# Silu in one activation, a third seven-product pair in every other feed-forward job, and the sums of down on VectorE

## The chip, the cores and the metric

The kernel runs on one core of one Trainium2 chip. A core has five engines with queues of their own: TensorE (PE in the rows; PEld are its weight loads), VectorE (DVE), ScalarE (ACT), GpSimd (POOL) and SyncE (SP, which here issues the loads of weights). Each takes its instructions in order. The metric is the device time of one execution, in microseconds; the time of before is the median of 3 runs.

## The reference

One decoder layer for 256 tokens of width 2048 in float32. Two mixers (a gated delta rule and a block attention) are merged by gates and projected; then comes a dense SwiGLU feed-forward, the part that the change touches:

```python
u = _rmsnorm(h, norm_ffn_w[l])
hid = jax.nn.silu(jnp.einsum('btd,df->btf', u, w_ffn_gate[l])) * jnp.einsum('btd,df->btf', u, w_ffn_up[l])
h = h + jnp.einsum('btf,fd->btd', hid, w_ffn_down[l])
```

with `D_FF` = 5632, so gate and up are 2048x5632 each and down is 5632x2048.

## The kernel before

**Float32 from three products.** TensorE multiplies operands of a shorter type (float32r). Each float32 tile is therefore held as two parts, hi (the tile cast to that type) and lo (what the cast left out). A product is three matmuls into the same bank: activation hi by weight hi (line 283), hi by lo (284), lo by hi (285). Weights come from HBM as units of 128x1024 (`wraw`). For each unit ScalarE casts `whi` (line 87) and VectorE subtracts `wlo` (line 88). Both have four buffers, and `get` asks for the parts three units ahead (`SPLIT_AHEAD`).

**Super jobs.** The feed-forward is 13 jobs: 11 for gate and up (512 columns of each side by side, `c` = 0 to 10) and 2 for down (1024 columns each). A job goes through its contraction in pairs of 128-row blocks: 8 pairs for gate and up, 22 for down. A pair is a 2x2 by 2x2 block product (two blocks of rows, two halves of the tokens, two blocks of columns). An ordinary pair needs 2 units of weights and 8 products (24 matmuls). A pair of *seven products* uses Winograd's form of Strassen's scheme: 21 matmuls on 4 units, of which two are built by VectorE from the loaded ones (lines 96, 97, 99 and 100, in place on `wraw`), one of 512 columns and three of 1024. It also needs sums of the activations: `make_sums` forms a sum of hi and lo (line 967) and four sums of quarters (970 to 973) on GpSimd, then ScalarE casts (975) and VectorE subtracts (976) the two parts. These sums are `usum` for gate and up, made once, and `dsum` for down, eight pairs. The products that seven-product pairs collect in four more banks (`pw`) are folded by `after` (lines 996 to 1000) on ScalarE and GpSimd behind the last such pair of a job.

Which pairs are of seven products, and in which order a job takes its pairs, stands in a table at the head of the program:

```python
FFN_PAIRS = (3, 5)
FFN_ORDER = [[0, 1, 2, 4, 6, 3, 5, 7]] + [list(range(KM // 2))] * (DFF // 512 - 1)
DOWN_PAIRS = (4, 8, 12, 15, 18, 2, 6, 10)
DOWN_USED = [(4, 8, 12, 15, 18), DOWN_PAIRS]
```

Job 0 thus has its two such pairs next to each other; in the other gate and up jobs pair 4 lies between 3 and 5.

**Side work.** While TensorE multiplies, short chains of other work are woven in, one step per `tick`, one or two ticks per pair's unit: `swiglu` of the job before (adds of the folded products, the activation, the products with up, 8 transposes, the split of `hid`), the sums of down, the output. The scheduler of the language then settles the order in which each engine gets its instructions; the order is fixed when the program is built. The second down job takes its last four units together (`last`).

Of the kernel before, what the change touches and what calls it, by code (L numbers as in the profile page):

```python
# [24 lines left out]
DFF = 5632  # L25
# [11 lines left out]

FFN_PAIRS = (3, 5)  # L40
FFN_ORDER = [[0, 1, 2, 4, 6, 3, 5, 7]] + [list(range(KM // 2))] * (DFF // 512 - 1)
DOWN_PAIRS = (4, 8, 12, 15, 18, 2, 6, 10)
DOWN_USED = [(4, 8, 12, 15, 18), DOWN_PAIRS]


def _super_jobs():

    jobs = [[(p, p in FFN_PAIRS) for p in order] for order in FFN_ORDER]
    return jobs + [[(p, p in used) for p in range(KF // 2)] for used in DOWN_USED]


# [61 lines left out]
def layer(ctx: ExitStack, tc: tile.TileContext, xT, xtok, params, consts, relt, w_bd, w, out):  # L113
    nc = tc.nc
# [25 lines left out]
    def small(name, shape, dtype=F32):  # L140
        return pools[-1].tile([P] + list(shape), dtype, name=name)
# [166 lines left out]
    with tc.tile_pool(name="xin", bufs=4) as xin:  # L308
# [597 lines left out]
    uT = acts.tile([P, KM, 512], F32R, name="uT", tag="actA")  # L906
# [23 lines left out]
        turn([h[:, n, fs] for n in range(NT)], weighted(j))  # L930
    low_stage.close()
    mid.close()
    r2h, r2q = small("r2h", [NT]), small("r2q", [NT])

    def h_scale():
        ss = small("hs", [NT])
        nc.vector.tensor_reduce(ss, hss, axis=AX.X, op=ALU.add)
        r2 = rsqrt("r2", ss, 1.0 / DM)
        nc.vector.tensor_scalar(r2h, r2, 0.5, None, op0=ALU.mult)
        nc.vector.tensor_mul(r2q, r2h, r2)  # L940
        yield

    chains.append(h_scale())


    low = acts.tile([P, H, 512], F32R, name="low", tag="actC")
    later = {}

    def hid(kc, n=1):
        t, k = (low, kc) if kc < H else (later["high"], kc - H)  # L950
        return t[:, k] if n == 1 else t[:, k:k + n]

    def fft(name, bufs):
        return later["ff"].tile([P, 512], F32, name=name, tag=name, bufs=bufs)
# [5 lines left out]
            nc.vector.tensor_sub(hid(4 * c, 4)[:, :, T + n * P:T + (n + 1) * P], p, hi.bitcast(F32))  # L960
        return evict

    def make_sums(g, c):

        c = c.bitcast(F32)
        f = fft("fsum", 2).rearrange("p (k t) -> p k t", k=2)
        nc.gpsimd.tensor_add(f, c[:, :, :T], c[:, :, T:])
        a11, a21, a12, a22 = f[:, 0, :P], f[:, 0, P:], f[:, 1, :P], f[:, 1, P:]
        t = fft("fsum", 2).rearrange("p (k t) -> p k t", k=4)
        nc.gpsimd.tensor_add(t[:, 0], a21, a22)  # L970
        nc.gpsimd.tensor_sub(t[:, 1], t[:, 0], a11)
        nc.gpsimd.tensor_sub(t[:, 2], a11, a21)
        nc.gpsimd.tensor_sub(t[:, 3], a12, t[:, 1])
        yield
        nc.scalar.copy(g[:, 0], t)
        nc.vector.tensor_sub(g[:, 1], t, g[:, 0].bitcast(F32))  # L976
        yield

    usums = {}

    def ffn_setup():
        by_stage.close()
        later["ff"] = ff = ctx.enter_context(tc.tile_pool(name="ff", bufs=1))
        later["high"] = ff.tile([P, KF - H, 512], F32R, name="high")
        yield
        for p in FFN_PAIRS:
            usums[p] = ff.tile([P, 2, 4, P], F32R, name="usum", tag="sum", bufs=2)
            yield from make_sums(usums[p], uT[:, 2 * p:2 * p + 2])

    parts = []  # L990

# [179 lines left out]
```

## Time and profile before

| | |
|---|---|
| median of 3 runs | 1475.7 us (1475.5 to 1476.75) |
| the profiled execution | 1475.54 us, of it 1473.8 us span of the profile |
| mean granted TensorE clock | 0.997 of full speed |
| TensorE busy | 1458.2 us, 99% of the span |
| VectorE, ScalarE, GpSimd busy | 73%, 52%, 14% |
| gate and up, then down | from about 763 us, from about 1230 us |

Durations of matmuls overlap, since they are pipelined, so their sum is no measure of how fast TensorE goes; distances between starts are.

### The profile page before, as it was taken

The numbers are of one execution on the slowest core, as the hardware profiler recorded it, in microseconds if no ns is written. First come the engines' busy times: TensorE is split into PE (matmuls) and PEld (weight loads), VectorE is DVE, ScalarE is ACT, GpSimd is POOL, SyncE is SP. The second block draws the span as 40 slices with busy tenths as digits, with TensorE's granted clock in tenths as the row PEclk, the third lists the DMA queues.
The fourth block names the chain that finished last, engine by engine and source line by source line (L and its number), as shares of the span: only waits on it lengthen the run. The fifth ranks groups of instructions, "written<-read, shape, count | busy, mean of one in ns | idle before, by whom it ended". The sixth has DMA issues, their size and how long they took to land.

```text
span 1473.8 us, 19231 instructions
## 1 busy us (share of the span) xinstructions
PE 1458.2 (99%) x7077; PEld 1213.5 (82%) x7077; DVE 1078.7 (73%) x1452; ACT 759.9 (52%) x1100; POOL 200.9 (14%) x148
## 2 busy tenths in 40 slices
PE   9999999999999999999999999999999999899998
PEld 8888788888888888888888888888888887688887
DVE  6887679777664455555569888888888887777885
ACT  6664446635454444444545555555555554444553
POOL 0011000020000000000021223022222116405003
PEclk9999999999999999999999999999999999899999
DMA  9457545575456666668756666565665556557763
GB/s 375 147 197 183 162 136 176 163 170 186 143 159 180 195 195 186 189 191 258 217 173 200 214 191 193 170 203 187 214 207 192 190 184 198 163 197 224 231 204 109
DMA packets 78735, 282.05 MB, mean 191 GB/s; under 512 B 8880, under 2 KB 9520, under 8 KB 78256
## 3 DMA queue, kind: packets, MB, share of 16 engines
q1 hardware_dynamic: 76032, 272.30, 59.3%
q0 software_dynamic: 1472, 5.24, 1.1%
q10 hardware_dynamic: 1136, 3.28, 1.0%
q8 instruction: 55, 0.90, 0.2%
q14 instruction: 40, 0.33, 0.1%
HBM read 276.46 MB, written 4.33 MB: 191 GB/s over the span
## 4 chain that ended last, share of the span: by engine, by line
PE 93%; DVE 3%; ACT 1%; issue 1%; POOL 1%; DMA 0%; SPq 0%; DVEq 0%; POOLq 0%; ACTq 0%
PE ps L283 13%; PE ps L284 13%; PE ps L285 13%; PE ps L218 11%; PE ps L219 11%; PE ps L220 11%; PE ps L199 6%; PE ps L200 3%; PE pw L284 2%; PE pw L285 2%; PE pw L283 2%; PE pT L299 1%; DVE wlo L88 1%; ACT whi L87 1%; DVE dsum L976 0%
## 5 line engine op out<-in xcount | busy, mean ns | idle before, releaser
L88 DVE TENSOR_TENSOR wlo<-wraw,whi 128x1024 fp32r<-128x1024 f32 (+1 forms) x575 | 702.8, 1236 | 282.1 <-ACT whi L87 277.0
L87 ACT CAST whi<-wraw 128x1024 fp32r<-128x1024 f32 (+1 forms) x575 | 585.3, 1025 | 604.2 <-PE ps L285 233.6
L283 PE MATMUL ps<-whi,uT 128*128 128x512 f32 x572 | 223.8, 391 | 0.7 <-ACT whi L87 0.7
L285 PE MATMUL ps<-whi,uT 128*128 128x512 f32 x572 | 222.8, 390 | 0.0
L284 PE MATMUL ps<-wlo,uT 128*128 128x512 f32 x572 | 222.8, 389 | 0.0
L218 PE MATMUL ps<-whi,aT 128*128 128x512 f32 x512 | 204.5, 400 | 0.0
L219 PE MATMUL ps<-wlo,aT 128*128 128x512 f32 x512 | 200.1, 391 | 0.1
L220 PE MATMUL ps<-whi,aT 128*128 128x512 f32 x512 | 199.8, 390 | 0.0
L199 PE MATMUL ps<-aT,whi 128*128 128x512 f32 x384 | 139.0, 405 | 1.7 <-DVE aT L333 1.7
L283 PEld LDWEIGHTS ps<-whi,uT 128*128 128x128 f32 x572 | 107.4, 188 | 23.0 <-ACT whi L87 1.1
L285 PEld LDWEIGHTS ps<-whi,uT 128*128 128x128 f32 x572 | 107.4, 188 | 22.6
L284 PEld LDWEIGHTS ps<-wlo,uT 128*128 128x128 f32 x572 | 107.4, 188 | 21.9
L220 PEld LDWEIGHTS ps<-whi,aT 128*128 128x128 f32 x512 | 96.1, 188 | 20.3
L218 PEld LDWEIGHTS ps<-whi,aT 128*128 128x128 f32 x512 | 96.3, 188 | 18.8
L219 PEld LDWEIGHTS ps<-wlo,aT 128*128 128x128 f32 x512 | 96.3, 188 | 18.5 <-DVE wlo L88 0.4
L200 PE MATMUL ps<-aT,wlo 128*128 128x256 f32 x384 | 108.4, 282 | 0.9 <-DVE wlo L88 0.9
L199 PEld LDWEIGHTS ps<-aT,whi 128*128 128x128 f32 x384 | 73.5, 192 | 18.5 <-DVE aT L333 2.0
L284 PE MATMUL ps<-wlo,high 128*128 128x512 f32 x216 | 84.7, 392 | 0.4 <-DVE wlo L88 0.4
L283 PE MATMUL ps<-whi,high 128*128 128x512 f32 x216 | 84.6, 392 | 0.0
L285 PE MATMUL ps<-whi,high 128*128 128x512 f32 x216 | 84.6, 392 | 0.0
L997 POOL TENSOR_TENSOR ft<-ft 128x512 f32<-128x512 f32 x13 | 23.5, 1805 | 446.7 <-ACT ft L996 446.7
L200 PEld LDWEIGHTS ps<-aT,wlo 128*128 128x128 f32 x384 | 73.8, 192 | 1.3 <-DVE wlo L88 1.2
(395 smaller groups left out, 2004.3 us busy)
## 6 DMA issues: line engine op xcount, KB each, us to landing
wraw<-in_w SPq DMA_DIRECT2D x503, 512.0 KB, 4.2
xrow<-in_xtok SPq DMA_DIRECT2D x1, 2048.0 KB, 13.7
lb<-dm ACTq DMA_DIRECT2D x2, 1024.0 KB
xr<-in_xtok SPq DMA_DIRECT2D x8, 256.0 KB, 6.9
hsave<-h POOLq DMA_DIRECT2D x4, 512.0 KB, 5.5
hx<-hsave POOLq DMA_DIRECT2D x4, 512.0 KB, 7.8
xc<-in_xT SPq DMA_DIRECT2D x3, 512.0 KB, 7.5
bias<-in_relt SPq DMA_DIRECT2D x4, 256.0 KB, 4.0
```

The source lines that it names most:

```text
L87: self.last_hi = self.nc.scalar.copy(hi[:, f], raw[:, f])
L88: self.last_lo = self.nc.vector.tensor_sub(lo[:, f], raw[:, f], hi[:, f].bitcast(F32))
L199: nc.tensor.matmul(ps[:, j], hi[:, sl], act[:, kc], start=kc == 0, stop=False)
L200: nc.tensor.matmul(ps[:, j, :T], lo[:, sl], act[:, kc, :T], start=False, stop=kc == nk - 1)
L218: nc.tensor.matmul(ps[n], ah, hi[:, sl], start=kc == 0, stop=False)
L219: nc.tensor.matmul(ps[n], ah, lo[:, sl], start=False, stop=False)
L220: nc.tensor.matmul(ps[n], al, hi[:, sl], start=False, stop=kc == nk - 1)
L283: nc.tensor.matmul(ps, ah, hi[:, sl], start=i == use[0], stop=False)
L284: nc.tensor.matmul(ps, ah, lo[:, sl], start=False, stop=False)
L285: nc.tensor.matmul(ps, al, hi[:, sl], start=False, stop=i == use[-1])
L299: nc.tensor.transpose(p[n][:, i], srcs[n][:, i * P:(i + 1) * P], ident)
L997: nc.gpsimd.tensor_add(t[2], t[0], t[2])
```

## The change

Three things. The gate's activation is `Silu` in one ScalarE instruction in place of `Tanh` and a VectorE instruction that made Silu of it; `r2h` and `r2q` become one `r2`. Gate and up jobs of odd number have three seven-product pairs (2, 4 and 5) in their natural order, those of even number two (2 and 5), with pair 3 taken before 2; down has six (7, 9, 11, 13, 15, 17) in its first job and these and 2 and 5 in its second. And the five operations of `make_sums` run on VectorE, in `ft` tiles for gate and up and in a tile `room2` for down, with a third buffer of the tag `sum`; the order within `make_sums` puts the cast ahead of the `yield`.

```diff
-FFN_PAIRS = (3, 5)
-FFN_ORDER = [[0, 1, 2, 4, 6, 3, 5, 7]] + [list(range(KM // 2))] * (DFF // 512 - 1)
-DOWN_PAIRS = (4, 8, 12, 15, 18, 2, 6, 10)
-DOWN_USED = [(4, 8, 12, 15, 18), DOWN_PAIRS]
+FFN_PAIRS = (2, 4, 5)
+FFN_USED = [(2, 5), (2, 4, 5)]
+FFN_ORDER = [[0, 1, 3, 4, 6, 2, 5, 7]] + [[0, 1, 2, 3, 4, 5, 6, 7], [0, 1, 3, 2, 4, 5, 6, 7]] * (DFF // 1024)
+DOWN_PAIRS = (7, 9, 11, 13, 15, 17, 2, 5)
+DOWN_USED = [DOWN_PAIRS[:6], DOWN_PAIRS]
...
-    jobs = [[(p, p in FFN_PAIRS) for p in order] for order in FFN_ORDER]
+    jobs = [[(p, p in FFN_USED[c % 2]) for p in order] for c, order in enumerate(FFN_ORDER)]
...
-        f = fft("fsum", 2).rearrange("p (k t) -> p k t", k=2)
-        nc.gpsimd.tensor_add(f, c[:, :, :T], c[:, :, T:])
+        f = f.rearrange("p (k t) -> p k t", k=2)
+        nc.vector.tensor_add(f, c[:, :, :T], c[:, :, T:])
         a11, a21, a12, a22 = f[:, 0, :P], f[:, 0, P:], f[:, 1, :P], f[:, 1, P:]
-        t = fft("fsum", 2).rearrange("p (k t) -> p k t", k=4)
-        nc.gpsimd.tensor_add(t[:, 0], a21, a22)
-        nc.gpsimd.tensor_sub(t[:, 1], t[:, 0], a11)
-        nc.gpsimd.tensor_sub(t[:, 2], a11, a21)
-        nc.gpsimd.tensor_sub(t[:, 3], a12, t[:, 1])
-        yield
+        t = t.rearrange("p (k t) -> p k t", k=4)
+        nc.vector.tensor_add(t[:, 0], a21, a22)
+        nc.vector.tensor_sub(t[:, 1], t[:, 0], a11)
+        nc.vector.tensor_sub(t[:, 2], a11, a21)
+        nc.vector.tensor_sub(t[:, 3], a12, t[:, 1])
         nc.scalar.copy(g[:, 0], t)
+        yield
         nc.vector.tensor_sub(g[:, 1], t, g[:, 0].bitcast(F32))
...
-            nc.scalar.activation(gs[n], t[2 * n], AF.Tanh, scale=r2h[:, n:n + 1])
+            nc.scalar.activation(gs[n], t[2 * n], AF.Silu, scale=r2[:, n:n + 1])
...
-            nc.vector.scalar_tensor_tensor(gs[n], gs[n], 1.0, t[2 * n], op0=ALU.add, op1=ALU.mult)
-        yield
-        for n in range(NT):
-            nc.vector.scalar_tensor_tensor(gs[n], t[2 * n + 1], r2q[:, n:n + 1], gs[n], op0=ALU.mult, op1=ALU.mult)
+            nc.vector.scalar_tensor_tensor(gs[n], t[2 * n + 1], r2[:, n:n + 1], gs[n], op0=ALU.mult, op1=ALU.mult)
...
+        room = later["ff"].tile([P, 2, 512], F32, name="room2", tag="sum", bufs=3)
         for i, p in enumerate(DOWN_PAIRS):
-            yield from make_sums(dsum[:, i], hid(2 * p, 2))
+            yield from make_sums(dsum[:, i], hid(2 * p, 2), room[:, 0], room[:, 1])
```

The line numbers of the changed program are one higher than before up to the sums, and differ by one to three behind them (88 is now 89 for `wlo`, 976 is 975, 960 is 959).

How the orders move, at three places. First, VectorE in gate and up job 1, from the split of `hid` of job 0 (`low`) on. Before, an ordinary pair's rows stand between the first seven-product pair and the second, and behind the second only ordinary weights follow:

```order
L960 TENSOR_TENSOR low<-pT,low 128x4x128 x2
L88 TENSOR_TENSOR wlo<-wraw,whi 128x1024 x3
L88 TENSOR_TENSOR wlo<-wraw,whi 128x512
L96 TENSOR_TENSOR wraw<-wraw 128x512
L88 TENSOR_TENSOR wlo<-wraw,whi 128x1024
L97 TENSOR_TENSOR wraw<-wraw 128x512
L99 TENSOR_TENSOR wraw<-wraw 128x512
L100 TENSOR_TENSOR wraw<-wraw 128x512
L88 TENSOR_TENSOR wlo<-wraw,whi 128x1024 x9
```

In the changed program, at the same place:

```order
L959 TENSOR_TENSOR low<-pT,low 128x4x128 x2
L89 TENSOR_TENSOR wlo<-wraw,whi 128x1024 x2
L89 TENSOR_TENSOR wlo<-wraw,whi 128x512
L97 TENSOR_TENSOR wraw<-wraw 128x512
L89 TENSOR_TENSOR wlo<-wraw,whi 128x1024
L98 TENSOR_TENSOR wraw<-wraw 128x512
L100 TENSOR_TENSOR wraw<-wraw 128x512
L101 TENSOR_TENSOR wraw<-wraw 128x512
L89 TENSOR_TENSOR wlo<-wraw,whi 128x1024 x2
L89 TENSOR_TENSOR wlo<-wraw,whi 128x512
L97 TENSOR_TENSOR wraw<-wraw 128x512
L89 TENSOR_TENSOR wlo<-wraw,whi 128x1024
```

The rows of pair 5 (the second group from `wlo` 128x512 on) now follow those of pair 4 directly.

Second, VectorE at the start of the first down job, from the end of `swiglu` of job 10 on. Before, it has one instruction per sum (`dsum`), and the first seven-product pair's weights (128x512, 96, 97) begin behind the third sum:

```order
L1016 SCALAR_TENSOR_TENSOR fg<-ft,r2q,fg 128x512 x2
L88 TENSOR_TENSOR wlo<-wraw,whi 128x1024
L976 TENSOR_TENSOR dsum<-fsum,dsum 128x512
L88 TENSOR_TENSOR wlo<-wraw,whi 128x1024
L976 TENSOR_TENSOR dsum<-fsum,dsum 128x512
L88 TENSOR_TENSOR wlo<-wraw,whi 128x1024
L976 TENSOR_TENSOR dsum<-fsum,dsum 128x512
L88 TENSOR_TENSOR wlo<-wraw,whi 128x512
L960 TENSOR_TENSOR high<-pT,high 128x4x128 x2
L96 TENSOR_TENSOR wraw<-wraw 128x512
L976 TENSOR_TENSOR dsum<-fsum,dsum 128x512
L97 TENSOR_TENSOR wraw<-wraw 128x512
```

In the changed program, from the same point on (`room` is the tile of the sums):

```order
L1012 SCALAR_TENSOR_TENSOR fg<-ft,r2s,fg 128x512 x2
L89 TENSOR_TENSOR wlo<-wraw,whi 128x1024
L975 TENSOR_TENSOR dsum<-room_10594,dsum 128x512
L969 TENSOR_TENSOR room_10594<-room_10594 128x128
L971 TENSOR_TENSOR room_10594<-room_10594 128x128
L970 TENSOR_TENSOR room_10594<-room_10594 128x128
L89 TENSOR_TENSOR wlo<-wraw,whi 128x1024
L972 TENSOR_TENSOR room_10594<-room_10594 128x128
L966 TENSOR_TENSOR room_10594<-high 128x512
L975 TENSOR_TENSOR dsum<-room_10594,dsum 128x512
L969 TENSOR_TENSOR room_10594<-room_10594 128x128
L971 TENSOR_TENSOR room_10594<-room_10594 128x128
```

Each sum's six VectorE instructions lie between the subtractions of ordinary weights, all eight sums ahead of the third unit of the first seven-product pair.

Third, ScalarE at the end of job 0, in the changed program:

```order
L995 COPY ft<-pw 128x512 x4
L88 CAST whi<-wraw 128x1024 x4
L1006 ACT_TABLE_LOAD
L1006 ACTIVATE fg<-ft,r2s 128x512 x2
L88 CAST whi<-wraw 128x512
```

Before, there is no table load at this place, only one at the start of the program; now there are these two in all.

## Rows read from the trace of the kernel before

**Rows 1.** Head of the profile: busy time, share of the span, instructions of TensorE.
```profile
PE 1458.2 (99%) x7077; PEld 1213.5 (82%) x7077; DVE 1078.7 (73%) x1452; ACT 759.9 (52%) x1100; POOL 200.9 (14%) x148
```

**Rows 2.** Timeline of TensorE in down: start, duration, line, operation.
```profile
1249.76 0.39 PE L283 MATMUL pw<-whi,high 128*128 128x512 f32 x1
...
1281.41 0.39 PE L283 MATMUL pw<-whi,high 128*128 128x512 f32 x1
...
1302.49 0.39 PE L283 MATMUL pw<-whi,high 128*128 128x512 f32 x1
...
1448.01 0.39 PE L283 MATMUL pw<-whi,high 128*128 128x512 f32 x1
...
1469.62 0.39 PE L285 MATMUL ps<-whi,high 128*128 128x512 f32 x1
```

**Rows 3.** Windows: stretch, length, busy us of each engine, PEclk, DMA share, GB/s.
```profile
1250.00:1266.00 16.00, 10.05 (x26) 6.40 (x25) 10.54 (x10) 5.48 (x7) 13.93 (x15) 0.68 0.27 79
1266.00:1291.00 25.00, 25.00 (x112) 20.67 (x111) 19.57 (x20) 13.45 (x15) 3.59 (x4) 1.00 0.69 210
```

**Rows 4.** All waits of TensorE after 800 us: total us, times, longest.
```profile
PE pw L284 <- DVE wlo L88: 3.3, 2, 2.6
PE ps L284 <- DVE wlo L88: 1.6, 2, 1.2
PE pw L283 <- ACT whi L87: 1.4, 1, 1.4
```

**Rows 5.** Timeline, first sums of down; in brackets idle time, releaser.
```profile
1252.05 0.50 PE L284 MATMUL ps<-wlo,dsum 128*128 128x512 f32 x1 [1.21 <-DVE wlo L88]
...
1253.29 0.62 ACT L975 CAST dsum<-fsum 128x512 fp32r<-128x512 f32 x1 [3.62 <-POOL fsum L973]
...
1253.94 1.21 DVE L976 TENSOR_TENSOR dsum<-fsum,dsum 128x512 fp32r<-128x512 f32 x1 [1.95 <-ACT dsum L975]
...
1259.54 1.23 DVE L976 TENSOR_TENSOR dsum<-fsum,dsum 128x512 fp32r<-128x512 f32 x1 [1.53 <-ACT dsum L975]
```

**Rows 6.** Groups by line and shape, VectorE: busy us, mean ns, idle before.
```profile
L88 DVE TENSOR_TENSOR wlo<-wraw,whi 128x1024 fp32r<-128x1024 f32 x538 | 678.6, 1273 | 264.1 <-ACT whi L87 259.0 <-DMA wraw<-in_w 1.5 <-PE pPT L829 0.6
...
L1013 DVE SCALAR_TENSOR_TENSOR fg<-fg,ft 128x512 f32<-128x512 f32 x22 | 14.5, 683 | 0.0
...
L606 DVE TENSOR_TENSOR prod<-lb,X 128x128 f32<-128x128 f32 x2 | 0.8, 394 | 0.1
...
L568 DVE TENSOR_TENSOR mc<-mc,cst 128x128 f32<-128x128 f32 x2 | 0.6, 280 | 0.0
```

**Rows 7.** Timelines of TensorE and VectorE in job 0, two neighbouring seven-product pairs.
```profile
779.34 0.39 PE L283 MATMUL pw<-whi,uT 128*128 128x512 f32 x1
...
787.62 0.50 PE L283 MATMUL ps<-whi,uT 128*128 128x512 f32 x1 [0.71 <-ACT whi L87]
...
809.06 1.04 PE L299 MATMUL pT<-ident,fg 128*128 128x128 f32 x8
...
780.67 1.83 DVE L88 TENSOR_TENSOR wlo<-wraw,whi 128x1024 fp32r<-128x1024 f32 x2 [0.26 <-ACT whi L87]
...
784.27 0.69 DVE L97 TENSOR_TENSOR wraw<-wraw 128x512 f32<-128x512 f32 x1
784.99 0.69 DVE L99 TENSOR_TENSOR wraw<-wraw 128x512 f32<-128x512 f32 x1
...
786.33 4.76 DVE L88 TENSOR_TENSOR wlo<-wraw,whi 128x1024 fp32r<-128x1024 f32 x4
```

**Rows 8.** The same in job 1, second seven-product pair.
```profile
822.90 0.39 PE L283 MATMUL pw<-whi,uT 128*128 128x512 f32 x1
...
824.23 3.61 DVE L88 TENSOR_TENSOR wlo<-wraw,whi 128x1024 fp32r<-128x1024 f32 x3 [0.66 <-ACT whi L87]
```

**Rows 9.** Groups by line and shape, ScalarE: busy us, mean ns, idle before.
```profile
L1007 ACT ACTIVATE fg<-ft,r2h 128x512 f32<-128x512 f32 x22 | 14.7, 715 | 3.1 <-DVE ft L1006 3.1
...
L321 ACT ACT_TABLE_LOAD x1 | 1.3, 1283 | 1.7 <-PEq L1162 1.7
```

More of the change, by code (lines that the diff above doesn't have):

```diff
@@ L932, in layer @@
     mid.close()
-    r2h, r2q = small("r2h", [NT]), small("r2q", [NT])
+    r2 = small("r2s", [NT])
     def h_scale():
@@ L937, in h_scale @@
         nc.vector.tensor_reduce(ss, hss, axis=AX.X, op=ALU.add)
-        r2 = rsqrt("r2", ss, 1.0 / DM)
-        nc.vector.tensor_scalar(r2h, r2, 0.5, None, op0=ALU.mult)
-        nc.vector.tensor_mul(r2q, r2h, r2)
+        nc.vector.tensor_copy(r2, rsqrt("r2", ss, 1.0 / DM))
         yield
@@ L961, in parted, with make_sums @@
         return evict
-    def make_sums(g, c):
+    def make_sums(g, c, f, t):
         c = c.bitcast(F32)
-        f = fft("fsum", 2).rearrange("p (k t) -> p k t", k=2)
-        nc.gpsimd.tensor_add(f, c[:, :, :T], c[:, :, T:])
+        f = f.rearrange("p (k t) -> p k t", k=2)
+        nc.vector.tensor_add(f, c[:, :, :T], c[:, :, T:])
         a11, a21, a12, a22 = f[:, 0, :P], f[:, 0, P:], f[:, 1, :P], f[:, 1, P:]
-        t = fft("fsum", 2).rearrange("p (k t) -> p k t", k=4)
-        nc.gpsimd.tensor_add(t[:, 0], a21, a22)
-        nc.gpsimd.tensor_sub(t[:, 1], t[:, 0], a11)
-        nc.gpsimd.tensor_sub(t[:, 2], a11, a21)
-        nc.gpsimd.tensor_sub(t[:, 3], a12, t[:, 1])
+        t = t.rearrange("p (k t) -> p k t", k=4)
[3 more added lines that the diff above has]
+        nc.vector.tensor_sub(t[:, 3], a12, t[:, 1])
+        nc.scalar.copy(g[:, 0], t)
         yield
-        nc.scalar.copy(g[:, 0], t)
         nc.vector.tensor_sub(g[:, 1], t, g[:, 0].bitcast(F32))
@@ L986, in ffn_setup @@
         for p in FFN_PAIRS:
-            usums[p] = ff.tile([P, 2, 4, P], F32R, name="usum", tag="sum", bufs=2)
-            yield from make_sums(usums[p], uT[:, 2 * p:2 * p + 2])
+            usums[p] = ff.tile([P, 2, 4, P], F32R, name="usum", tag="sum", bufs=3)
+            yield from make_sums(usums[p], uT[:, 2 * p:2 * p + 2], fft("ft", 4), fft("ft", 4))
     parts = []
@@ L1048, in layer @@
     for j in range(2):
-        hx = [later["ff"].tile([P, NT, 512], F32, name="hx", tag="sum", bufs=2) for _ in range(2)]
+        hx = [later["ff"].tile([P, NT, 512], F32, name="hx", tag="sum", bufs=3) for _ in range(2)]
         for f in range(2):
```

## The prediction

> **What bounds the kernel now.** I read the head of the profile first: TensorE is busy for 99% of the span [rows 1], so time can only come from fewer matmuls or from stretches in which matmuls run late. The busy figure cannot show lateness, since durations of pipelined matmuls overlap. The timeline can: count the matmuls between two points, and multiply by the undisturbed pitch. In the first down job the seven-product pairs 8 and 12 begin at 1281.41 and 1302.49 us [rows 2]; between them lie one pair of seven products (21 matmuls) and three ordinary pairs (24 each), 93 matmuls in 21.08 us, or 0.2267 us each. That is the price of a matmul here, not the 0.39 us that a row shows.
>
> The same ruler finds the late places. Pair 4 begins at 1249.76 us; from there to pair 8 there are again 93 matmuls, but they take 31.65 us [rows 2]: **10.57 us are lost at the first sums of down.** The windows agree: TensorE is busy 10.05 of 16 us there, and the mean granted clock falls to 0.68, so part of the stretch ran at the lower of its two levels, 1.2 GHz [rows 3]. Last, the list of TensorE's waits has only five after 800 us, all on weight halves (`whi`, `wlo`) [rows 4]; the first is at 1252.05 us. The timeline there says why: ScalarE's next instruction is a cast of a sum (`dsum`, L975) that waits 3.62 us for GpSimd, and VectorE's for the same sum waits 1.95 us for ScalarE [rows 5]; the weight casts (L87) and subtractions (L88) that TensorE needs are queued behind these two. One lap of this chain takes 5.6 us (1253.94 to 1259.54), too long for two laps in a seven-product pair.
>
> **The products.** An ordinary pair is 8 products of 3 matmuls, a seven-product pair 7. Now there are 11×2 + 5 + 8 = 35 such pairs; then 6×2 + 5×3 + 6 + 8 = 41. Six pairs more remove 18 matmuls: 18 × 0.2267 = **−4.08 us**.
>
> **The sums of down.** GpSimd's five operations per sum become VectorE's: one of 128x512 at 0.69 us (as L97) [rows 7] and four of 128x128. Rows of that size lie at 0.280 (L568) and 0.394 us (L606) [rows 6]; I take 0.33, the middle. A sum thus adds 2.0 us to VectorE, and the cast no longer waits for another engine's queue. The first such pair is now pair 7, not 4, so eight sums have 14 ordinary units of weights (two per pair, 12 × 0.2267 = 2.72 us each) in which to be made. Is VectorE fast enough? From the start of the job to the third unit of that pair, TensorE needs 14 × 12 + 9 = 177 matmuls, 40.1 us, and 0.9 us of transposes: 41.0 us. The order of rows gives VectorE in that stretch, at 1.18 us from start to start for a weight subtraction (four run in 4.76 us) [rows 7]: 12 of units 2 to 13 (14.2), the old job's rest (8 of 512, 5.5), eight `dsum` (5.5), six sums of 512 (4.1), 28 small ones (9.2), and the pair's own work to its third unit (5.9): 44.4 us. It starts with the first finished bank of the job before, about 1.9 us (8 matmuls) early, so it is ready at 42.5: 1.5 us late, or 0.1 if the small ones take 0.28, or 3.3 at 0.394. I take **0.7 us** of remaining wait, about halfway between the first two. So −10.57 + 0.7 = **−9.9 us**. If the sums held the queues as long as now, the gain would be 0.
>
> **The third pair in every other feed-forward job.** Jobs 1, 3, 5, 7 and 9 have pairs 2, 4 and 5, and 4 and 5 are neighbours. A seven-product pair gives TensorE 21 × 0.2267 = 4.76 us, but costs VectorE about 0.69 + 3 × 1.18 + 4 × 0.72 = 7.1 us [rows 7]. A single one is absorbed: after 800 us no job's pair made TensorE wait, as they stand one ordinary pair apart. But job 0 already has two neighbours, and there the trace shows the price. The first begins at 779.34 and the next transposes at 809.06, with 126 matmuls (42 + 24 + 60) between: 29.72 − 28.56 = **1.16 us late**, with a visible wait on `whi` at 787.62 [rows 7]. The mechanism is a chain from the four buffers of `whi`: the first pair's fourth unit cannot be cast before TensorE leaves the last ordinary unit. VectorE starts its subtraction at 780.67, 1.33 us after the pair's start, and from there works through the second pair's changes of weights to 786.33, where the third unit's subtraction starts. That is ready at 787.5, while TensorE would want it after 21 + 9 matmuls, at 786.14.
>
> Would jobs 1 to 9 be any better? In job 1 of before, the second pair's fourth unit starts on VectorE 1.33 us after that pair's start too (822.90, 824.23), with VectorE idle 0.66 us ahead of it [rows 8], after one ordinary pair, as in the change. So the chain begins at the same point with no debt, and runs the same operations in the same order. I take 1.16 us five times: **+5.8 us**. The bounds are 0, if TensorE's reordering hides it, and 2.8 us each, if VectorE's debt from the earlier pair (7.1 − 4.76 = 2.3 us) is not worked off. The third pair is therefore a bad bargain: 3.4 us of products (15 matmuls) for 5.8 us of waits. Job 0 keeps its neighbours (2 and 5 now), and its own sums, three on VectorE, fill gaps there: 0, with up to 1 us more.
>
> **Silu.** Two VectorE operations per job vanish (22 × 0.683 = 15 us of VectorE's time) [rows 6], at the start of a job, where nothing waits for VectorE now: 0 on the path. No row shows Silu; the nearest is Tanh at 0.715 us for the same shape and the same pointer scale [rows 9], and plain casts are 0.6. Even 1 us more would only shorten a margin. In ScalarE's order one table load appears, ahead of the first Silu in job 1, and none after. A load took 1.283 us at the start [rows 9]; in job 1 VectorE's second subtraction has a us of slack behind it: 0, bounded by 1.3. The Trainium skill, "ScalarE: Activation LUTs", section "What ACT_TABLE_LOAD costs", adds a drain of about 1.38 us, 2.66 us for a switch; no run here shows that drain, and by that price the same bound would be 2.7 us, once.
>
> **Nothing for the rest.** The 93 matmuls from pair 18's start (1448.01) on end at about 1469.85, one pitch after the last start, 0.76 us late [rows 2]. The change ends GpSimd's additions a pair earlier there, but the last four units are still fetched together: 0, at best −0.76. The third `sum` buffer and the earlier load of `hx` lie on GpSimd's queue, which waits for ScalarE anyway.
>
> **Sum.** −4.08 − 9.9 + 5.8 = −8.2 us. The profiled execution took 1475.54 us (span 1473.8), 0.2 below the median of the runs shown: 1475.54 − 8.2 = **1467.3 us**.
>
> **Rivals.**
> 1. *The neighbours cost nothing* (TensorE finds other matmuls, or the shorter VectorE list in these jobs helps): −4.08 − 9.9 = −14.0, so **1461.6**. Against it: job 0 has the same chain. Chance 0.14.
> 2. *VectorE is late with more than this*: with 3.3 us at the sums and 2 us for each of the five, −14.65 + 3.3 + 10 = −1.4, **1474**; milder mixes give 1470 and up. For it: 44.4 us of work in 41. Chance 0.17.
> 3. *VectorE pays for emptying its pipe behind every operation.* The timeline speaks against it: dependent operations of 0.69 us start 0.72 us apart (784.27 and 784.99 us) [rows 7]. Were each of the eight sums 1.2 us longer, 9.6 us of the gain would be lost, and the time **1476.9**. Chance 0.03. The Trainium skill, "VectorE: DVE Perf Modes", section "The DRAIN you can't avoid", states such a flush of about the operation's time less 266 ns; these rows show none between starts.
> 4. *Slower*: the waits at the neighbours let the granted clock fall, as in the first down job. It decides from (14.65 − 0.7) / 5 = 2.8 us per job. If each wait of 1.16 us also brought 16 matmuls at half the clock (16 × 0.2267 = 3.6 us more), it would be 4.8 us a job: −14.0 + 24 = +10, **1485**. Against it: job 0's 1.16 us is measured 20 us behind its wait and holds whatever the clock did; the low clock stands where four waits come together [rows 3, 4]. Chance 0.07.
>
> **Chances.** My forecast (1464.5 to 1470) has 0.55, and 0.04 lies between the cases. About 0.2%, 3 us, is what a measurement of this kernel can tell from no change. Faster takes the forecast, rival 1, the better part of rival 2 (0.1) and the rest: 0.83; same, the other part of rival 2 and most of rival 3: 0.09; slower: 0.08. The range reaches down over rival 1 and up to rival 2's worst: 1461 to 1473.
>
> **What the new profile would show.** Right: no TensorE wait between the start of down and its end but for one under 1 us at pair 7; no clock below 1.00 there; in jobs 1, 3, 5, 7, 9 one wait each on `whi` or `wlo` in pair 5, and distances that are about 1.2 us over the count; 18 matmuls fewer. Wrong: odd jobs that keep to the count; waits on `dsum` or the weight halves in the first down job; several table loads; half clock after pair 5.

## The result and the profile after

The changed kernel takes **1467.68 us** (median of 4 runs, 1467.31 to 1470.37) against 1476.14 us before (4 runs, 1475.5 to 1476.75): a ratio of 0.9947, 95% interval 0.9929 to 0.9964. The forecast was 1467.3 us. The profiled execution of the changed kernel is its longest, 1470.37 us with a span of 1468.6 us. It lost time ahead of the change: a group of four transposes of `h`, which stands 12 matmuls into gate and up job 0, starts 2.86 us later than in the profile of before, although TensorE's 3930 matmuls and transposes ahead of it are the same in both programs.

These transposes in TensorE's timeline of before:

```profile
753.80 0.60 PE L299 MATMUL pT<-ident,h 128*128 128x128 f32 x4
```

And TensorE's timeline after, from the same transposes to the last matmul, with jobs 0 and 1 and the first seven-product pair of down between, which answers to [rows 2, 7, 8]:

```profile
756.66 0.60 PE L300 MATMUL pT<-ident,h 128*128 128x128 f32 x4
...
782.18 0.39 PE L284 MATMUL pw<-whi,uT 128*128 128x512 f32 x1
...
809.19 1.03 PE L300 MATMUL pT<-ident,fg 128*128 128x128 f32 x8
...
813.95 0.50 PE L284 MATMUL pw<-whi,usum 128*128 128x512 f32 x1 [0.99 <-DVE low L959]
...
821.57 0.39 PE L284 MATMUL pw<-whi,uT 128*128 128x512 f32 x1
...
826.33 0.39 PE L284 MATMUL pw<-whi,uT 128*128 128x512 f32 x1
...
829.84 0.50 PE L284 MATMUL pw<-whi,usum 128*128 128x512 f32 x1 [0.69 <-ACT whi L88]
...
854.02 0.60 PE L300 MATMUL pT<-ident,fg 128*128 128x128 f32 x4
...
1217.30 0.39 PE L284 MATMUL pw<-whi,uT 128*128 128x512 f32 x1
...
1271.92 0.39 PE L284 MATMUL pw<-whi,high 128*128 128x512 f32 x1
...
1464.44 0.39 PE L286 MATMUL ps<-whi,high 128*128 128x512 f32 x1
```

From the first of these rows to the start of the last matmul, before takes 1469.62 [rows 2] - 753.80 = 715.82 us, after 1464.44 - 756.66 = 707.78 us: **8.04 us less, where the prediction's sum says 8.2**. I compare this stretch from here on, since it leaves out a part that the change doesn't touch and that differs between executions (what is known of it stands at the end of the account of the prediction).

With the prediction's ruler of 0.2267 us per matmul: job 0 has 114 matmuls from 782.18 to the transposes, 25.84 us, and takes 27.01, so 1.17 us are lost at its neighbours, as before. In job 1, 117 matmuls from pair 5 (826.33) on are 26.52 us and take 27.69: 1.17 lost. Job 3's (913.01 to 940.68) lose 1.15. From 1217.30 up to the first seven-product pair of down at 1271.92 there are 237 matmuls and 8 transposes, 53.73 and some 0.87 us, in 54.62: nothing is lost. The surprise is in job 1 ahead of the neighbours. The row of 813.95 lies in its first seven-product pair, which begins behind the transposes at 809.98. From there 45 matmuls, 10.20 us, take until 821.57: **1.39 us lost, once**.

The head of the profile after, which answers to [rows 1], has 18 matmuls less, 69 more instructions on VectorE and 50 fewer on GpSimd:

```profile
PE 1452.2 (99%) x7059; PEld 1207.2 (82%) x7059; DVE 1109.0 (76%) x1521; ACT 772.3 (53%) x1114; POOL 157.4 (11%) x98
```

All waits of TensorE after 780 us (total us, times, longest), which answer to [rows 4]:

```profile
PE pw L284 <- ACT whi L88: 3.5, 5, 0.7
PE pw L284 <- DVE low L959: 1.0, 1, 1.0
PE ps L284 <- ACT whi L88: 0.7, 1, 0.7
PE ps L285 <- DVE wlo L89: 0.7, 1, 0.7
```

The first row is the five odd jobs, one wait each. The third is job 0, the fourth the last units of the program; at both places before had one too. The second, on the split of `hid` (`low`), was not foreseen: those matmuls write a bank that still holds the transposes until VectorE has split them. Nothing is left in the first down job, where the windows (stretch, length, busy us of each engine, granted clock, DMA share, GB/s), which answer to [rows 3], now show a full TensorE at full clock and a VectorE with hardly a gap:

```profile
1254.00:1272.00 18.00, 18.00 (x81) 14.91 (x80) 17.72 (x36) 8.26 (x11) 0.72 (x1) 1.00 0.54 163
1272.00:1291.00 19.00, 19.00 (x86) 15.73 (x85) 17.59 (x20) 11.44 (x12) 0.00 (x0) 1.00 0.75 249
```

### The profile page after: what moved, and what is told of

Same layout as the page of the kernel before. It is cut to its first block, busy times and chain, and to the rows that moved or that the text cites. A ratio compares the mean times of both kernels' runs of the same rounds, so it can differ in the third digit from the quotient of the medians.

```text
span 1468.6 us, 19242 instructions
## 1 busy us (share of the span) xinstructions
PE 1452.2 (99%) x7059; PEld 1207.2 (82%) x7059; DVE 1109.0 (76%) x1521; ACT 772.3 (53%) x1114; POOL 157.4 (11%) x98
## 4 chain that ended last, share of the span: by engine, by line
PE 85%; DVE 6%; DMA 3%; ACT 2%; issue 2%; POOL 0%; ACTq 0%; SPq 0%; DVEq 0%; POOLq 0%
PE ps L285 13%; PE ps L286 13%; PE ps L284 13%; PE ps L219 9%; PE ps L220 9%; PE ps L221 9%; PE ps L200 5%; DMA lb<-dm 3%; PE ps L201 3%; DVE wlo L89 2%; PE pw L285 2%; PE pw L286 2%; PE pw L284 2%; ACT whi L88 2%; PE pT L300 1%
## 5 line engine op out<-in xcount | busy, mean ns | idle before, releaser
L89 DVE TENSOR_TENSOR wlo<-wraw,whi 128x1024 fp32r<-128x1024 f32 (+1 forms) x587 | 717.5, 1240 | 261.3 <-ACT whi L88 259.0
L88 ACT CAST whi<-wraw 128x1024 fp32r<-128x1024 f32 (+1 forms) x587 | 594.2, 1023 | 596.6 <-PE ps L221 228.1
L284 PE MATMUL ps<-whi,uT 128*128 128x512 f32 x542 | 212.0, 391 | 0.7 <-ACT whi L88 0.7
L286 PE MATMUL ps<-whi,uT 128*128 128x512 f32 x542 | 211.0, 389 | 0.0
L285 PE MATMUL ps<-wlo,uT 128*128 128x512 f32 x542 | 211.0, 389 | 0.0
L284 PEld LDWEIGHTS ps<-whi,uT 128*128 128x128 f32 x542 | 101.8, 188 | 21.9 <-ACT whi L88 1.1
L286 PEld LDWEIGHTS ps<-whi,uT 128*128 128x128 f32 x542 | 101.7, 188 | 21.3
L285 PEld LDWEIGHTS ps<-wlo,uT 128*128 128x128 f32 x542 | 101.8, 188 | 20.8
L286 PE MATMUL ps<-whi,high 128*128 128x512 f32 x210 | 81.7, 389 | 0.0
L284 PE MATMUL ps<-whi,high 128*128 128x512 f32 x210 | 81.5, 389 | 0.0
```

The source lines that it names most:

```text
L88: self.last_hi = self.nc.scalar.copy(hi[:, f], raw[:, f])
L89: self.last_lo = self.nc.vector.tensor_sub(lo[:, f], raw[:, f], hi[:, f].bitcast(F32))
L284: nc.tensor.matmul(ps, ah, hi[:, sl], start=i == use[0], stop=False)
L285: nc.tensor.matmul(ps, ah, lo[:, sl], start=False, stop=False)
L286: nc.tensor.matmul(ps, al, hi[:, sl], start=False, stop=i == use[-1])
```

## The experiments

All are compared over the same stretch, so that each number has a trace behind it, and by their medians. "Less" and "more" below are differences of the stretch. The kernel before ran on the same chip as each of them: 1474.01 us (9 runs) beside the first four, 1474.73 (9) beside the next four, 1474.56 (16) beside the last two.

| kernel | median us (runs) | ratio to before, 95% interval | stretch, us | against before |
|---|---|---|---|---|
| before | 1476.14 (4) | | 715.82 | |
| after | 1467.68 (4) | 0.9947, 0.9929 to 0.9964 | 707.78 | -8.04 |
| e1_two_pairs | 1462.16 (4) | 0.9918, 0.9904 to 0.9931 | 704.14 | -11.68 |
| e2_apart | 1460.37 (4) | 0.9910, 0.9895 to 0.9925 | 702.02 | -13.80 |
| e3_table_early | 1468.37 (5) | 0.9961, 0.9949 to 0.9974 | 708.83 | -6.99 |
| e4_gpsimd_sums | 1480.28 (5) | 1.0040, 1.0027 to 1.0052 | 720.96 | +5.14 |
| e5_vector_sums | 1463.80 (4) | 0.9922, 0.9907 to 0.9937 | 705.28 | -10.54 |
| e6_five_whi | 1468.05 (6) | 0.9951, 0.9936 to 0.9966 | 705.62 | -10.20 |
| e7_job0 | 1466.18 (4) | 0.9942, 0.9927 to 0.9956 | 706.88 | -8.94 |
| e8_apart_job0 | 1460.05 (4) | 0.9900, 0.9885 to 0.9914 | 701.15 | -14.67 |
| e9_silu_only | 1476.72 (11) | 1.0010, 1.0001 to 1.0019 | 717.54 | +1.72 |
| e10_three_apart | 1469.55 (6) | 0.9970, 0.9958 to 0.9981 | 710.27 | -5.55 |

**The third pair, taken away (e1).** My theory: the third pair costs more than its products give. The rival: what is lost in odd jobs is lost at the products, not at the neighbours.

```diff
-FFN_USED = [(2, 5), (2, 4, 5)]
+FFN_USED = [(2, 5), (2, 5)]
-FFN_ORDER = ... [[0, 1, 2, 3, 4, 5, 6, 7], [0, 1, 3, 2, 4, 5, 6, 7]] ...
+FFN_ORDER = ... [[0, 1, 3, 2, 4, 5, 6, 7], [0, 1, 3, 2, 4, 5, 6, 7]] ...
```

> Every gate and up job takes two seven-product pairs, 2 and 5, with one ordinary pair between them (job 0 keeps its neighbours). My theory: each of the five odd jobs loses a wait of 1.16 us and gets 3 matmuls back (0.68 us), so 5 x (1.16 - 0.68) = 2.4 us faster than the changed kernel, about 1465.2 us, and no wait on whi inside jobs 1 to 10. Rival: the wait comes with any job's seven-product pairs and not with neighbours; then the 15 matmuls come on top, 3.4 us slower, about 1471.

Measured: 3.64 us less than after. The neighbours' five waits are gone (two of 0.7 us are left, in job 0 and at the end), and job 1's wait on `low` with them, since its first seven-product pair now comes one pair later. That second effect is the excess over the forecast: five times 1.16 less 15 x 0.2267 = 3.40 gives 2.4, and job 1's 1.39 makes it 3.8, where 3.64 was measured.

**The third pair, kept but apart (e2).** The order alone decides, if neighbours are the cause:

```diff
-[0, 1, 2, 3, 4, 5, 6, 7]
+[0, 1, 2, 3, 4, 6, 5, 7]
```

> The odd jobs keep three seven-product pairs, but take pair 6 between 4 and 5 (positions 2, 4 and 6 of 8). My theory: no neighbours, no waits, so 5 x 1.16 = 5.8 us faster than the changed kernel, about 1461.9. Rival: the folded products' four additions on GpSimd (some 8.4 us behind four copies) now have only one ordinary pair, 5.4 us, until the job ends; VectorE's first add of the next job waits up to 5 us for them, and the weight subtractions queued behind it make TensorE wait: no gain, or up to 5 us a job slower (1468 to 1490).

Measured: 5.76 us less than after. The five waits are gone, job 1's is not:

```profile
PE pw L284 <- DVE low L959: 1.0, 1, 1.0
PE ps L284 <- ACT whi L88: 0.7, 1, 0.7
PE ps L285 <- DVE wlo L89: 0.7, 1, 0.7
```

So the third pair is not bad by itself. Here one ordinary pair between two seven-product pairs pays for both, as the prediction read from before; the place made it a loss.

**A fifth buffer of `whi` (e6).** The mechanism that the prediction gave for the neighbours is a chain from the four buffers of `whi`. The fifth buffer took the room of one buffer of `wraw`.

```diff
-RAW = 7
+RAW = 6
-        hi = self.pool.tile([P, 1024], F32R, name="whi", tag="whi", bufs=4)
+        hi = self.pool.tile([P, 1024], F32R, name="whi", tag="whi", bufs=5)
```

> The changed kernel with five buffers of whi instead of four, paid for by six wraw buffers instead of seven. My theory: the wait at neighbours is a chain that starts when TensorE leaves the last ordinary unit, first the cast, then the subtraction; with a fifth whi buffer the cast is done ahead and only the wlo buffer holds, so VectorE starts 0.7 to 1.1 us earlier and the six waits shrink from 1.16 to 0.1 to 0.5 us each: 4 to 6 us less from the first seven-product pair to the end. Rival: VectorE's rate alone sets the wait; it stays at 1.16 us.

Measured: the neighbours' loss is gone. In job 1, pair 5 begins at 831.37 and the transposes at 858.01: 26.64 us for 26.52 of matmuls, 0.12 late instead of 1.17; in job 3, 917.20 to 943.86, 0.14. Job 0 is no longer late either (789.43 to 810.61: 21.18 us for 93 matmuls, 21.08). But one wait has grown, and nothing else is left in the list of waits after 780 us:

```profile
PE pw L284 <- DVE low L959: 3.0, 1, 3.0
```

So the gain over the stretch is 2.16 us in place of about 7, and the whole program gains nothing: the stretch starts at 758.95 us, later than in any other trace. Most of that delay arises in one place, a wait of 1.74 us on VectorE ahead of 346.61 us and a stretch of low clock behind it; whether the smaller `RAW` brings this, no run shows. The wait on `low` brought the low clock too (last section).

**What makes job 1 late: the table load, or the fold (e3, e7).** Ahead of the wait on `low`, ScalarE loads the table for Silu (1.283 us at 799.58), and VectorE's adds of `swiglu` wait for GpSimd's last add of the fold. VectorE's timeline in the changed kernel:

```profile
795.23 5.71 DVE L89 TENSOR_TENSOR wlo<-wraw,whi 128x1024 fp32r<-128x1024 f32 x3 [1.29 <-ACT whi L88]
800.86 0.68 DVE L1005 TENSOR_TENSOR ft<-ft,ps 128x512 f32<-128x512 f32 x1
802.13 0.69 DVE L1005 TENSOR_TENSOR ft<-ft,ps 128x512 f32<-128x512 f32 x1 [0.60 <-POOL ft L999]
...
810.79 2.51 DVE L89 TENSOR_TENSOR wlo<-wraw,whi 128x1024 fp32r<-128x1024 f32 x2
813.21 1.28 DVE L959 TENSOR_TENSOR low<-pT,low 128x512 fp32r<-128x512 f32 x2
```

My first theory was the load. In e3 a small activation (128x2), early in job 0, moves it ahead of the job:

```diff
+        nc.scalar.activation(warm, r2, AF.Silu)
```

> One more Silu of two elements per partition right behind the scale r2, at the start of job 0, so that the table is loaded there. My theory: the 0.99 us wait of TensorE in job 1 on the split of hid (low), and with it 1.4 us against the count of matmuls, comes from the table load of 1.28 us ahead of the first Silu; it goes, 1.3 us faster than the changed kernel, about 1466.4. Rivals: with the drain that a page adds, 2.7 us, 1465.0; or the wait is due to the three pairs of job 1 and stays, 1467.7.

Measured: 1.05 us *more* than after, and the wait on `low` is 1.99 us, not gone. **The theory fell**: the load had been hidden. What grew is seen on VectorE and on ScalarE in e3:

```profile
806.06 1.22 DVE L89 TENSOR_TENSOR wlo<-wraw,whi 128x1024 fp32r<-128x1024 f32 x1
807.19 0.68 DVE L101 TENSOR_TENSOR wraw<-wraw 128x512 f32<-128x512 f32 x1
809.07 1.22 DVE L89 TENSOR_TENSOR wlo<-wraw,whi 128x1024 fp32r<-128x1024 f32 x1 [1.19 <-ACT whi L88]
810.21 1.28 DVE L960 TENSOR_TENSOR low<-pT,low 128x512 fp32r<-128x512 f32 x2
```
```profile
807.99 1.05 ACT L88 CAST whi<-wraw 128x1024 fp32r<-128x1024 f32 x1 [2.54 <-DVE wraw L101]
808.94 1.06 ACT L959 CAST low<-pT 128x512 fp32r<-128x512 f32 x2
```

In both kernels the split of `hid` (`low`) stands behind the fourth unit of the seven-product pair, on both engines. What e3 changed is VectorE's order ahead of it: the third unit's subtraction (806.06) now comes before the last change of weights (L101, 807.19), where the changed kernel makes it behind. The fourth unit's cast can only start when that change is made, and its subtraction waits for the cast, with VectorE idle for 1.19 us. The split and TensorE's bank wait behind them. In e6 the same order is there (a subtraction with 1.19 us of idle time at 814.27, the split at 816.55). How late the split is sets the wait: it starts 4.02 us behind the transposes in the changed kernel (809.19, 813.21), 5.02 in e3 and 5.95 in e6, and TensorE waits 0.99, 1.99 and 3.01 us.

In e7 job 0 makes its first seven-product pair one place earlier and its last one, so the fold starts earlier:

```diff
-FFN_ORDER = [[0, 1, 3, 4, 6, 2, 5, 7]] + ...
+FFN_ORDER = [[0, 1, 3, 2, 4, 5, 6, 7]] + ...
```

> The changed kernel with job 0 in the order of the even jobs, pairs 2 and 5 at positions 3 and 5 of 8. My theory: the neighbours' 1.16 us in job 0 goes, and since the fold of job 0 on GpSimd ends a pair earlier, VectorE's adds at the start of job 1 no longer wait for it, so the 1.4 us of job 1 go too: 2.5 us less. Rivals: the sums of pair 2 aren't ready at position 3 and TensorE waits for them (up to 3 us); or job 1's loss comes from its own three pairs and stays (1.2 us less).

Measured: 0.90 us less than after; the forecast was too high. Job 1's loss is gone (806.95 to 817.25: 10.30 us for 10.20), so an earlier end of job 0's pair and fold is enough to remove it. The split still stands behind the fourth unit, but starts 2.47 us behind the transposes (806.16, 808.63), as in the later jobs of the changed kernel. So its place in the order is no loss as long as VectorE reaches it in time. But job 0 itself became 0.4 us longer (753.22 to 806.16, 52.94 us; after 756.66 to 809.19, 52.53), though its pairs are now apart. A likely reason is that the first of them comes while VectorE still makes the sums of gate and up (the last `usum` at 775.55 us, behind the pair's start at 767.86). Two waits of 0.20 and 0.56 us on `whi` replace one of 0.71.

**Both orders (e8).** With e2's and e7's edits together:

> Both orders together: odd jobs with pair 6 between 4 and 5, job 0 in the order of the even jobs. My theory: no seven-product pairs are neighbours anywhere in gate and up, so of the waits after the first pair only the 0.7 us at the end is left: 5.8 + 2.5 = 8.3 us less than the changed kernel from the first such pair to the end, about 1459. Rival: job 1's 1.4 us stays, 6.9 us less.

Measured: 6.63 us less than after, against 5.76 + 0.90 = 6.66 from the two apart. The sum is near the rival's 6.9, but not for its reason: job 1's loss is gone, and job 0's is not (751.86 to 804.79, 52.93 us, as in e7). It has the shortest stretch of all and is 1.0% faster than before; by the intervals of its time it can't be told from e2. The only waits left in it are two in job 0, 0.8 us together, and 0.7 at the end.

**The third pair everywhere (e10).** If apart is enough, the even jobs 2 to 10 could have a third pair as well:

```diff
-    jobs = [[(p, p in FFN_USED[c % 2]) ...
+    jobs = [[(p, p in FFN_USED[c > 0]) ...
-FFN_ORDER = ... [[0, 1, 2, 3, 4, 6, 5, 7], [0, 1, 3, 2, 4, 5, 6, 7]] * (DFF // 1024)
+FFN_ORDER = ... [[0, 1, 2, 3, 4, 6, 5, 7]] * (DFF // 512 - 1)
```

> The best kernel so far (pairs 4 and 5 apart in the odd jobs, job 0 with its second seven-product pair one place earlier) with the third seven-product pair in the even jobs 2 to 10 as well, in the same order 0, 1, 2, 3, 4, 6, 5, 7: 15 matmuls fewer. My theory is that only neighbours cost time, and one ordinary pair between two seven-product pairs is enough: 15 x 0.2267 = 3.4 us less than the kernel it is made from (1460.05 us), about 1456.7 us, with no new wait of TensorE between 830 us and down. Rival: three such pairs in every job fill VectorE, since the pair at position 6 is followed by the next job's pair at position 2 after only three ordinary pairs, with the swiglu and the eviction of the old job in between; then a wait on whi, wlo or low comes in most of the ten jobs, at 0.7 to 1.2 us each 7 to 12 us, and the time is 1463 us or more.

Measured: 9.12 us *more* than e8, with 15 matmuls fewer. My theory fell, the rival holds: 3.40 us of matmuls saved and 12.5 lost. The two largest groups of TensorE's waits in it, and VectorE between two jobs:

```profile
PE pT L300 <- DVE high L959: 3.6, 4, 0.9
PE pw L284 <- DVE high L959: 2.9, 4, 0.7
```
```profile
848.27 2.50 DVE L89 TENSOR_TENSOR wlo<-wraw,whi 128x1024 fp32r<-128x1024 f32 x2
850.69 0.68 DVE L959 TENSOR_TENSOR low<-pT,low 128x512 fp32r<-128x512 f32 x1
```

Here the split of `hid` is late in every gate and up job from job 2 on: it starts 3.50 us behind job 2's transposes (847.19, 850.69) and 3.74 behind job 3's (891.05, 894.79), where job 1's starts 2.46 behind. Distances from transposes to transposes show the price: 804.82 to 847.19 is 42.37 us, no loss (183 matmuls, 41.49, and the transposes); the next, 847.19 to 891.05, is 43.86, and the one behind it 43.41. VectorE's share of the time from 860 to 1230 us is 88% (324.72 of 370 us), where after has 87% (321.37 of 370): its total load hardly tells them apart, so the order is the likelier cause.

**Sums on VectorE (e5, e4).** e5 is the kernel before with the five operations of `make_sums` on VectorE and the cast ahead of the `yield`, and nothing else; e4 is the changed kernel with these five back on GpSimd.

```diff
-        nc.gpsimd.tensor_add(f, c[:, :, :T], c[:, :, T:])
+        nc.vector.tensor_add(f, c[:, :, :T], c[:, :, T:])
...
-        nc.gpsimd.tensor_sub(t[:, 3], a12, t[:, 1])
-        yield
+        nc.vector.tensor_sub(t[:, 3], a12, t[:, 1])
         nc.scalar.copy(g[:, 0], t)
+        yield
```

> The kernel before with one part of the change: the five operations of each sum on VectorE, and the cast ahead of the yield. Tables (first seven-product pair of down is 4) and Tanh stay. My theory: the sums no longer hold ScalarE's queue for GpSimd, so most of the 10.57 us come back; VectorE has only 8 ordinary units instead of 14 before the first seven-product pair, so some 2 to 4 us of waits stay: 6 to 9 us faster than before. Rival: the later first pair is what the change gains by; then nothing, within 2 us of before.

> The five operations of each sum go back to GpSimd; the tables of pairs, Silu and the order of cast and yield stay as changed. My theory: ScalarE's casts wait for GpSimd again and hold the weight casts, so TensorE loses about the 10 us of before at the start of down, about 1477. Rival: what helped is the table, whose first seven-product pair of down is now 7 and not 4, some 16 us later; then at most 2 us are lost, 1468 to 1470.

Measured: e5 gains 10.54 us over before, which is the loss of 10.57 [rows 2] to 0.03 us, so the sums alone give more than the whole change. The 2 to 4 us of waits that I expected did not come: from the first seven-product pair of down to the second (1248.91 to 1269.99) its 93 matmuls take 21.08 us, their bare price. e4 loses 13.2 us against after: 2.1 ahead of job 0's seven-product pairs (753.39 to 781.05, 27.66 us; after 25.52) and 10.4 up to the first one of down (1216.82 to 1281.82, 65.00 us; after 54.62). ScalarE there, in e4:

```profile
1254.58 0.62 ACT L973 CAST dsum<-room 128x512 fp32r<-128x512 f32 x1 [2.21 <-POOL room L972]
1255.10 1.04 ACT L88 CAST whi<-wraw 128x1024 fp32r<-128x1024 f32 x1
1259.32 0.62 ACT L973 CAST dsum<-room 128x512 fp32r<-128x512 f32 x1 [3.18 <-POOL room L972]
```

The lap is 4.74 us with one weight unit in each, and TensorE wants one every 2.72 us. That is the coupling of queues that the prediction described, and it also tells that neither the later first pair (7 for 4) nor the cast's new place removed the loss, since e4 has both. The engine was needed; whether it would have been enough without the cast's new place, no run shows.

**Silu alone (e9).** The kernel before with the edits of the activation only:

```diff
-            nc.scalar.activation(gs[n], t[2 * n], AF.Tanh, scale=r2h[:, n:n + 1])
+            nc.scalar.activation(gs[n], t[2 * n], AF.Silu, scale=r2[:, n:n + 1])
...
-            nc.vector.scalar_tensor_tensor(gs[n], gs[n], 1.0, t[2 * n], op0=ALU.add, op1=ALU.mult)
```

> The kernel before with Silu alone (one activation with the whole scale, three instead of four VectorE operations per row block of the swiglu); pairs, orders and GpSimd's sums as before. My theory: 22 x 0.683 = 15 us of VectorE's time go, none of it on the path, and the one table load in job 1 is hidden, so the time stays within 1 us of the kernel before, ratio 0.999 to 1.001, and the stretch from the last transposes ahead of the feed-forward part (753.80 us in the profile of before) to the last matmul stays within 0.5 us of 715.82 us. Rival a: the table load and what comes with it hold up TensorE once: 1.3 to 2.7 us more, with a wait in job 1 that before did not have. Rival b: the shorter list lets VectorE begin the first sum of down earlier; the last job's rest is then 2 x 0.68 us shorter ahead of the chain of sums, and up to 1.4 us come off the 10.57 us that are lost there.

Measured: 1.72 us more, though no new wait came in job 1, so rival a is out, and b has the wrong sign. Up to the first seven-product pair of down the kernel is 0.67 us ahead of before (495.29 us from the transposes on, before 495.96); from there to the second one it takes 34.08 us, where before took 31.65 [rows 2]. The loss is in the stretch where GpSimd makes the sums:

```profile
1249.00:1265.00 16.00, 8.99 (x21) 5.01 (x20) 11.02 (x10) 5.64 (x7) 13.44 (x15) 0.66 0.14 40
1265.00:1291.00 26.00, 26.00 (x110) 21.38 (x109) 18.32 (x18) 13.73 (x15) 1.06 (x3) 0.95 0.65 209
```

TensorE is busy 1 us less in 16 than in [rows 3], and the low clock reaches into the second window. Which step makes the chain worse was not followed; that the shorter `swiglu` moves the queues against each other there is not shown. In the changed kernel that chain is gone, so nothing of this remains in it.

## Why the prediction held, point by point

**The products, -4.08 us**: 18 matmuls fewer, as counted. **The sums, -9.9**: the gain is 10.57, since the 0.7 us of remaining wait did not come. The mean of three of the four small operations is longer than the 0.33 us that I took (L970 and L972 are as L969):

```profile
L969 DVE TENSOR_TENSOR room<-room 128x128 f32<-128x128 f32 x8 | 3.4, 429 | 0.2
...
L971 DVE TENSOR_TENSOR room<-room 128x128 f32<-128x128 f32 x8 | 2.3, 284 | 0.0
```

But the mean misleads: it comes from one long operation in each of the three, ahead of the stretch that I summed (last section). All others took 0.28 or 0.29 us, and they start 0.20 to 0.32 us apart. In a sum without other work between, they take from 1254.86 to 1255.80, 0.94 us or 0.24 each, so even less than the 0.28 for which the prediction's working leaves 0.1 us of wait. The step that was off is the middle value of 0.33. Rival 3 is out too: nothing is lost here, and a next operation starts 0.20 us behind the start of one of 0.28 us, so no flush stands between them.

**The neighbours, +5.8**: five times 1.14 to 1.17 us, as job 0 had shown, and the step that gives the cause is confirmed: apart (e2) or with a fifth buffer (e6) they cost nothing. Rivals 1 and 2 are out. Rival 4 did not come either: the granted clock stayed at 1.00 through all five waits of 0.7 us. Behind a wait of 3.01 us it did fall, in e6 (last section).

**Silu, 0**: in the changed kernel the table load stands in ScalarE's order in job 1, and ScalarE waits 0.71 us for VectorE behind it anyway; e3, which moves it away, does not get faster. Silu itself takes what Tanh took [rows 9]:

```profile
L1006 ACT ACTIVATE fg<-ft,r2s 128x512 f32<-128x512 f32 x22 | 14.8, 717 | 2.6 <-DVE ft L1005 2.6
...
L1006 ACT ACT_TABLE_LOAD x1 | 1.3, 1283 | 0.0
```

The Trainium skill, "ScalarE: Activation LUTs", section "What ACT_TABLE_LOAD costs", puts a drain of about 1.38 us on top of such a load. The traces show the load's 1283 ns but no drain. In the changed kernel the load starts 0.02 us behind the cast ahead of it, and Silu starts 0.71 us behind the load, just when the add that it waits for has ended. In e8 no wait hides anything, and Silu follows at once:

```profile
794.10 1.06 ACT L88 CAST whi<-wraw 128x1024 fp32r<-128x1024 f32 x1 [1.67 <-PE ps L286]
795.18 1.28 ACT L1006 ACT_TABLE_LOAD   x1
796.48 1.34 ACT L1006 ACTIVATE fg<-ft,r2s 128x512 f32<-128x512 f32 x2
```

From the cast's end (795.16) to Silu's start are 1.32 us, so by these rows the switch cost what the load took, and not the page's sum; of the prediction's two bounds 1.3 us was the right one.

**Job 0 and the tail, 0**: job 0's neighbours lose 1.17 us (1.16 before); from the tail's last seven-product pair (1437.16) 116 matmuls, 26.30 us, take 27.28, so 0.98 are lost where before lost 0.76.

**What the sum left out** is job 1's 1.39 us. The prediction looked at what seven-product pairs cost VectorE one behind the other, but not at what stands in the same queues at a job's start: the fold, `swiglu` and the split of `hid` of the old job. Pair 2 at the third place of job 1 comes before that is done, and only in job 1, since job 0 makes its own pairs late. Both moves take the loss away: pair 2 one place later (e1), or job 0's pairs earlier (e7). In the other direction, the transposes of two jobs and what surrounds them cost 2.0 us before (86.33 us from 809.06 to 895.39, less 372 x 0.2267) and 1.9 after (86.66 from 897.16 to 983.82, less 369 x 0.2267 and 1.15). Five times that is some 0.7 us.

The terms as measured: -4.08 - 10.57 + 5.8 + 1.39 + 0.2 - 0.7 = -8.0, which is the stretch's 8.04. That the forecast's 8.2 is so near is partly luck: what was left out or too low, 1.39 and 0.2, and what was too high or left out on the other side, 0.7 and 0.7, nearly cancel.

The part ahead of the stretch ends anywhere from 750.41 (e1) to 756.66 us (after) in ten traces with the same work there (all but e3 and e6), and two sources can be read off. First, the start of the program: a pair of TensorE's matmuls (512 and 256 columns) takes 0.64 us there and 0.35 later. In before and after this changes at about 13 us, while e1 has 0.35 from its second pair on (7.51 us). So the matmul that starts at 15.51 us in before starts at 15.63 in after and at 12.96 in e1. Second, two places (154.69 and 343.94 us in before) where TensorE waits for VectorE's `E`. Both waits together are 0.4 us in before, none in e1, and in after:

```profile
PE pD L624 <- DVE E L616: 2.1, 2, 1.1
```

Left open is why VectorE comes to these places later in some executions, and why the early matmuls of some go slower for longer.

## What to carry to other kernels

Count instructions between two starts and multiply by the undisturbed pitch; the lateness that this shows is the price list for a change that repeats the same pattern elsewhere, and here it held to 0.02 us in each of five jobs (1.14 to 1.17 us, 1.16 forecast). An operation that saves the busiest engine work can lose it again by where it stands: put such pieces apart, and look at what the old job still has in the queues before one is put near its start. Taking a chain off a slower engine's queue can be worth more than all savings in work (10.57 us against 4.08 here), so look first for a chain in which each step waits for another engine's queue.

## What the hardware showed that I had not expected

**VectorE and GpSimd hold each other up.** An add of 128x128 takes VectorE 0.28 us, but beside each of GpSimd's additions of the fold one takes 1.34 to 1.39 us, and ends just behind it. VectorE and GpSimd in the changed kernel, same stretch:

```profile
1223.78 1.39 DVE L969 TENSOR_TENSOR room<-room 128x128 f32<-128x128 f32 x1
1225.09 0.28 DVE L971 TENSOR_TENSOR room<-room 128x128 f32<-128x128 f32 x1
1225.29 1.38 DVE L970 TENSOR_TENSOR room<-room 128x128 f32<-128x128 f32 x1
1226.70 1.34 DVE L972 TENSOR_TENSOR room<-room 128x128 f32<-128x128 f32 x1
```
```profile
1223.13 1.89 POOL L996 TENSOR_TENSOR ft<-ft 128x512 f32<-128x512 f32 x1 [10.75 <-ACT ft L995]
1225.10 1.42 POOL L997 TENSOR_TENSOR ft<-ft 128x512 f32<-128x512 f32 x1
1226.60 1.29 POOL L998 TENSOR_TENSOR ft<-ft 128x512 f32<-128x512 f32 x1
```

GpSimd's ends are 1225.02, 1226.52 and 1227.89 us, VectorE's 1225.17, 1226.67 and 1228.04, each 0.15 us later. One such operation among eight, 1.4 for 0.28, makes a mean of (7 x 0.28 + 1.4) / 8 = 0.42: that is the whole of the surplus. The Trainium skill, "SBUF — State Buffer", section "Who interferes with whom", says that a VectorE instruction with two inputs in SBUF contends with a GpSimd instruction that reads SBUF, and calls the ports that the two engines share an exclusive lock. The rows agree, and so does the fold of job 0: beside the three subtractions of 795.23 us, which take 5.71 us where four took 4.77 at 789.17, GpSimd's additions take 2.16 to 2.35 us each, against 1.29 for the one ahead of them (793.90). It may be a part of what the sums cost on GpSimd, since they ran beside VectorE's subtractions; no run here parts it from the coupling of queues.

**A low clock can follow one wait alone.** In e6, TensorE ran without a gap up to job 1's wait of 3.01 us, and behind it the granted clock was 0.66 in the mean of 5 us: matmuls start 0.43 us apart from 818.62 to 822.02 us, which is the 1.2 GHz level. The windows ahead of and behind the wait:

```profile
809.00:814.30 5.30, 5.30 (x28) 4.21 (x26) 4.07 (x6) 2.16 (x3) 0.00 (x0) 1.00 0.18 34
817.30:822.30 5.00, 4.92 (x15) 3.90 (x16) 4.35 (x6) 1.37 (x2) 0.00 (x0) 0.66 0.81 280
```

The same trace has a second case: a wait of 1.74 us ends at 346.61 us, and the granted clock is 0.50 from 347.6 to 351.0. In before, waits of 1.21 and 1.44 us (ending at 1252.05 and 1254.91) stand right ahead of the fall at 1255.7. In e4 ten waits of 0.47 to 0.96 us came one behind the other (ending from 1256.20 to 1276.43 us, TensorE busy 13.64 of these 20.23), and the clock stayed at 1.00. Lateness in these smaller pieces cost only itself.
